# A two-layer trunk on one core: the second FFN's gate and up by seven block products

## The chip, the cores and the metric

The kernel runs on one core of a Trainium2 chip, in one launch. The metric is the device time of an execution in microseconds (us): for the kernel before, the median of three runs on the chip. In profiles PE is TensorE's matrix multiply and PEld its weight load, DVE is VectorE, ACT is ScalarE, POOL is GpSimd, and SP is SyncE, which issues the transfers (DMAs).

## The reference

A trunk of two layers on 1024 tokens with 1024 features, all in float32. Layer 0 is an S5 state-space mixer, layer 1 a dilated attention; each is followed by a SwiGLU FFN whose hidden width is 2816 (22 tiles of 128). The change touches the end of layer 1.

```python
def rmsnorm(x, g):
    xf = x.astype(jnp.float32)
    y = xf * lax.rsqrt(jnp.mean(xf * xf, axis=-1, keepdims=True) + RMS_EPS)
    return (y * g.astype(jnp.float32)).astype(x.dtype)

def swiglu(xn, w_gate_up, w_down):
    gate, up = jnp.split(xn @ w_gate_up, 2, axis=-1)
    return (jax.nn.silu(gate) * up) @ w_down

for layer in range(DEPTH):                   # 2 layers
    xn = rmsnorm(h, norm_mix[layer])
    ...                                      # y: S5 mixer, or dilated attention with x @ w_o at its end
    h = h + y.astype(h.dtype)
    h = h + swiglu(rmsnorm(h, norm_ffn[layer]), ffn_w_gate_up[layer], ffn_w_down[layer]).astype(h.dtype)
return rmsnorm(h, norm_final)
```

## The kernel before

**Number format.** Every float32 operand of a large product is split in two: a part `hi` rounded to the format fp32r, and the rest, `lo = x - hi`. ScalarE makes `hi` (a copy) and VectorE makes `lo` (a subtraction). A product is then three matmuls (`mm3`): hi·hi, hi·lo and lo·hi, from lines L244 to L246 of the profile. A matmul takes a 128x128 weight tile and a moving tile of 128x512.

**Tiling.** Activations lie feature by feature: a tile `128x1024` is one block of 128 features for all tokens, and its two halves (`hf`) are tokens 0 to 511 and 512 to 1023. Layer 1's end runs in four stages. The attention's *output projection* makes the eight feature blocks `f` of `h` (features 0 to 2 are mostly done inside the attention, whose order is planned apart); `residual` adds the old `h`, splits the sum into `HH` and `HL`, transposes it on TensorE (`ht`) and stores it by tokens in DRAM (`htok`), and collects the squares in `acc`. The *second FFN's gate and up* (`gate_up`) runs over 22 units `m`: each loads two weight tiles of 512 KB (`load_w`: transfer, GpSimd multiplies the norm's gain `g` in, ScalarE `whi`, VectorE `wlo`) and makes 2 x 2 products of 8 x 3 matmuls, 96 in all. After that VectorE multiplies by the norm factor `rb`, ScalarE takes silu, and GpSimd multiplies gate by up into `hid`, which stays on chip. In unit 0 the statistics come in: `st` sums the squares (`rstd_compact`), `rb` spreads the factor over the partitions (`rstd_bcast`). The *last down projection* (`fin`) runs over two halves of the output features and 11 chunks of two hidden tiles; `down_chunk` loads a piece of `w_down` and splits it (`dwh`, `dwl`) and the two hidden tiles (`sh`, `sl`). The *final norm* follows.

**The first FFN already works by blocks.** There `gate_up_blocks` cuts the product of a unit in 2 x 2 blocks: the weights by halves of the input features (first or second 512) and by gate or up, the activations by halves of features and of tokens. Seven block products of 4 x 3 matmuls take the place of eight: the left sides A11, A12, S1, S2, S3, A22, S4 are made for each unit by `a_blocks` (sums by GpSimd on L1037 and the lines behind it, splits by `a_split`, L1023), and the right sides B11, T1, B21, T2, T3, T4, B22 are made once, four tiles each, in the stage before (`b_first`, `b_second`, `bsplit` on L895). Of the 22 hidden tiles the first 16 are stored to DRAM and loaded again in the down projection.

**Order.** Outside the attention no order is written by hand: the program is handed to a scheduler that sets a row for each instruction on each engine, and an engine works its rows in that order. Tiles come from pools with a few buffers a tag (`whi` and `wlo` have three each), and a tile's first writer waits for the last reader of the tile that held the buffer before.

Of the kernel before, what the change touches and what calls it, by code (L numbers as in the profile page):

```python
# [18 lines left out]
NT = 8  # L19
# [151 lines left out]
def trunk(tc, a, out):  # L171
# [813 lines left out]
    def first_gu(layer):  # L985
        return [load_w(w_cols(a["ffn_w_gate_up"][layer], DFF * vg), g_ffn[layer], spare=vg == 1) for vg in range(2)]

    def gate_up(layer, acc, first=(), beside=None):
        w = a["ffn_w_gate_up"][layer]
        g = g_ffn[layer]  # L990
        first = list(first)
        hid = []
        rb = None
        for m in range(NF):
            ps = [[PB("gu") for _ in range(2)] for _ in range(2)]
            wx = []
            for vg in range(2):
                wx.append(first.pop(0) if first else load_w(w_cols(w, DFF * vg + 128 * m), g))
            st = {}
            if m == 0:  # L1000
                st = {KS: lambda: st.update(r=rstd_compact(acc, f"ffn{layer}")),
                      KR: lambda: st.update(b=rstd_bcast(st["r"], f"ffn{layer}"))}
# [10 lines left out]
            if beside and m in beside:  # L1013
                with tc.issue_after(last.ins):
                    beside[m]()
        return hid

    def a_split(name, src):
        where = ASPOT[name]
# [6 lines left out]
    ASPOT = {"A11": "whi", "S1": "wlo", "A12": "z", "S2": "z", "S3": "whi", "A22": "wlo", "S4": "z"}  # L1026

    def a_blocks(w, m):
# [9 lines left out]
        t["A11"] = a_split("A11", a11)  # L1038
        t["S1"] = a_split("S1", sf)
        G.tensor_sub(sf, sf, a11)  # L1040
        t["A12"] = a_split("A12", a12)
        t["S2"] = a_split("S2", sf)
        G.tensor_sub(a21, a11, a21)
        G.tensor_sub(a12, a12, sf)
        t["S3"] = a_split("S3", a21)
        t["A22"] = a_split("A22", a22)
        t["S4"] = a_split("S4", a12)
        return t

    def gate_up_blocks(layer, acc, beside=None):  # L1050

        w = a["ffn_w_gate_up"][layer]
# [3 lines left out]
        for m in range(NF):  # L1056
            t = a_blocks(w, m)
# [39 lines left out]
        return hid, hdram  # L1097
# [22 lines left out]
    def residual(f, ps, acc, tag, vf=(), tok=None):  # L1120
# [3 lines left out]
        for hf in range(2):  # L1124
# [8 lines left out]
            if tok is not None:  # L1133
                p = bank(tok, "ht")
# [530 lines left out]
    for m in range(NT):  # L1665
# [5 lines left out]
        for hf in range(2):  # L1671
            for k in ks_:
                o_mms(ps, w, hf, k)
# [72 lines left out]
```

## Time and profile before

| what | us |
|---|---|
| median of three runs (lowest, highest) | 2410.17 (2409.41, 2410.5) |
| the profiled execution | 2412.11 |
| its span in the trace | 2409.7 |
| the output projection, features 3 to 7 | about 1618 to 1680 |
| second FFN, gate and up: first to last matmul start | 1680.3 to 2162.5 |
| last down projection and final norm | to 2409.7 |
| first FFN, gate and up by blocks: first to last matmul start | 364.6 to 792.4 |

The profiled execution is one run of its own. All times in the rows are microseconds from the start of its span, and a row's engine is busy from its first instruction's start to its last one's end; TensorE's matmuls overlap in its pipeline, so that one shows 0.39 us while the next starts 0.23 us after it.

### The profile page before, as it was taken

Reading aid. Unit: us, or ns where it says so; the run is one execution under the profiler, and the core shown is the slowest. Engines: PE = TensorE matmul, PEld = TensorE weight load, DVE = VectorE, ACT = ScalarE, POOL = GpSimd, SP = SyncE. Lnnn points to the kernel's source line nnn. Section 1 sums busy time; section 2 is a strip of 40 time slices with the busy share of each in tenths; the row PEclk is TensorE's granted clock in tenths of the full one; section 3 lists DMA queues with packets and bytes.
Section 4 is the critical chain, followed back from the end, with each engine's and each line's share of the span. In section 5 each row is a group of like instructions: output and inputs, shape, how many; then the busy total and the mean of one; then the engine's idle time right before and its main releaser. Section 6 shows DMA issues by size and latency. Waiting matters only on the chain. (4 is left out here: it accounts for less than half of the span.)

```text
span 2409.7 us, 31977 instructions
## 1 busy us (share of the span) xinstructions
PE 2316.1 (96%) x12688; PEld 1960.4 (81%) x12688; DVE 1313.6 (55%) x2210; ACT 890.2 (37%) x1685; POOL 724.9 (30%) x581
## 2 busy tenths in 40 slices
PE   4779999999999999999999999999999999999998
PEld 3668887888888888889898989778888888888887
DVE  9994357766666435365667676656232323233434
ACT  7523334333333324255566565544111111113333
POOL 6661246666655001032112110115223222310100
PEclk9879999999999999999999999999999999999999
DMA  5213222222222521111111111324111111122112
GB/s 142 86 47 88 89 88 75 84 79 79 88 79 66 206 76 56 53 53 33 40 36 45 45 36 45 114 79 118 40 44 53 44 53 51 46 99 68 44 53 87
DMA packets 199319, 168.93 MB, mean 70 GB/s; under 512 B 18185, under 2 KB 171009, under 8 KB 199170
## 3 DMA queue, kind: packets, MB, share of 16 engines
q1 hardware_dynamic: 197154, 159.56, 20.9%
q0 software_dynamic: 2016, 7.34, 0.9%
q8 instruction: 99, 1.62, 0.3%
q14 instruction: 50, 0.41, 0.1%
HBM read 133.32 MB, written 33.55 MB: 69 GB/s over the span
## 5 line engine op out<-in xcount | busy, mean ns | idle before, releaser
L245 PE MATMUL gu<-hl,whi 128*128 128x512 f32 x704 | 274.1, 389 | 0.0
L244 PE MATMUL gu<-hh,whi 128*128 128x512 f32 x704 | 274.0, 389 | 0.0
L246 PE MATMUL gu<-hh,wlo 128*128 128x512 f32 x704 | 274.0, 389 | 0.0
L244 PE MATMUL pqk<-whi,hh 128*128 128x256 f32 x768 | 233.4, 304 | 1.2 <-ACT nat L1354 1.2
L246 PE MATMUL pqk<-whi,hl 128*128 128x256 f32 x768 | 217.4, 283 | 2.2 <-DVE hl L1132 2.2
L245 PE MATMUL pqk<-wlo,hh 128*128 128x256 f32 x768 | 217.4, 283 | 0.0
L209 ACT ACTIVATE whi<-wraw 128x1024 fp32r<-128x1024 f32 x92 | 97.1, 1059 | 312.9 <-PE gu L245 254.9
L234 POOL TENSOR_TENSOR wraw<-wraw,vec 128x1024 f32<-128x1024 f32 x46 | 88.2, 1917 | 348.0 <-DMA wraw<-in_ffn_w_gate_up_dram 197.3
L1112 DVE TENSOR_TENSOR dwl<-wraw,dwh 128x512 fp32r<-128x512 f32 x86 | 63.5, 741 | 225.5 <-ACT dwh L209 216.5
L244 PEld LDWEIGHTS pqk<-whi,hh 128*128 128x128 f32 x768 | 146.9, 191 | 18.5 <-issue 15.1
L209 ACT ACTIVATE dwh<-wraw 128x512 fp32r<-128x512 f32 x86 | 53.9, 629 | 279.4 <-PE fin L245 135.7
L244 PEld LDWEIGHTS gu<-hh,whi 128*128 128x128 f32 x704 | 132.1, 188 | 27.6
L246 PEld LDWEIGHTS gu<-hh,wlo 128*128 128x128 f32 x704 | 132.1, 188 | 27.3
L245 PEld LDWEIGHTS gu<-hl,whi 128*128 128x128 f32 x704 | 132.1, 188 | 27.3
L246 PEld LDWEIGHTS pqk<-whi,hl 128*128 128x128 f32 x768 | 146.6, 191 | 2.4 <-DVE hl L1132 2.4
L245 PEld LDWEIGHTS pqk<-wlo,hh 128*128 128x128 f32 x768 | 147.0, 191 | 0.0
L1469 DVE TENSOR_TENSOR pl<-ptp,ph 128x512 fp32r<-128x512 f32 (+1 forms) x160 | 100.2, 635 | 75.6 <-ACT ph L209 73.9
L245 PE MATMUL dn<-sl,dwh 128*128 128x512 f32 x352 | 136.6, 389 | 0.0
L244 PE MATMUL dn<-sh,dwh 128*128 128x512 f32 x352 | 135.3, 390 | 1.0 <-DVE dtmp L1126 1.0
L246 PE MATMUL dn<-sh,dwl 128*128 128x512 f32 x352 | 134.7, 389 | 0.0
L236 DVE TENSOR_TENSOR wlo<-wraw,whi 128x1024 fp32r<-128x1024 f32 x65 | 105.4, 1624 | 52.9 <-ACT whi L209 50.1
L244 PE MATMUL fin<-dwh,sh 128*128 128x512 f32 x336 | 130.7, 389 | 0.0
(1179 smaller groups left out, 5937.4 us busy)
## 6 DMA issues: line engine op xcount, KB each, us to landing
wraw<-in_ffn_w_gate_up_dram SPq DMA_DIRECT2D x88, 512.0 KB, 3.8
wraw<-in_ffn_w_down_dram SPq DMA_DIRECT2D x44, 512.0 KB, 3.3
wraw<-in_s_w_glu_dram SPq DMA_DIRECT2D x16, 512.0 KB, 4.0
hidd<-hid SPq DMA_DIRECT2D x16, 512.0 KB, 2.6
hd<-hidd SPq DMA_DIRECT2D x16, 512.0 KB, 8.1
wraw<-in_dil_w_qkv_dram SPq DMA_DIRECT2D x32, 256.0 KB, 3.3
x<-in_x_dram SPq DMA_DIRECT2D x8, 512.0 KB, 7.3
xts<-xT SPq DMA_DIRECT2D x8, 512.0 KB, 3.1
```

The source lines that it names most:

```text
L209: A.activation(o, i, AF.Copy)
L234: G.tensor_tensor(r3, r3, g.unsqueeze(2).to_broadcast([128, view[0], view[1]]), op=ALU.mult)
L236: V.tensor_sub(lo, raw, hi.bitcast(F32))
L244: T.matmul(ps, lh, rh, start=first, stop=False)
L245: T.matmul(ps, lh, rl, start=False, stop=False)
L246: T.matmul(ps, ll, rh, start=False, stop=last)
L1112: V.tensor_sub(wl, half(raw, i), wh.bitcast(F32))
L1469: V.tensor_sub(o_, i_, (t["ph"][:, :, 1] if part else t["ph"]).bitcast(F32))
```

## The change

The second FFN's gate and up go through `gate_up_blocks` as well, and `gate_up` falls away. The activations' blocks are made while the output projection runs, by the new function `residual_x` and the lines behind it. In the second layer the gain goes into the activations, the norm factor of the up half is left out in the units and multiplied in by VectorE at the end, when the down projection's result is added to `h`; 16 hidden tiles are stored and loaded again, and the down projection begins with tiles 16 to 21.

```diff
-    def first_gu(layer):
-        return [load_w(w_cols(a["ffn_w_gate_up"][layer], DFF * vg), g_ffn[layer], spare=vg == 1) for vg in range(2)]
-
-    def gate_up(layer, acc, first=(), beside=None):
-        w = a["ffn_w_gate_up"][layer]
-        g = g_ffn[layer]
-        first = list(first)
...
-        for m in range(NF):
-            ps = [[PB("gu") for _ in range(2)] for _ in range(2)]
-            wx = []
-            for vg in range(2):
...
-            unit_mms(ps, wx, HH, HL, m == 0, dict(st))
-            rb = st["b"] if m == 0 else rb
-            hd = Z4(f"hid{layer}_{m}") if m < 16 else B4(f"hid{layer}_{m}")
-            for hf in range(2):
-                s_ = T2("s_")
-                V.tensor_mul(s_, ps[hf][0], half(rb, hf))
-                last = V.tensor_mul(half(hd, hf), ps[hf][1], half(rb, hf))
-                A.activation(s_, s_, AF.Silu)
-                G.tensor_mul(half(hd, hf), half(hd, hf), s_)
-            hid.append(hd)
...
+    def a_split(name, src, layer):
+        where = ASPOT[layer][name]
         nm = uid(name)
-        t = Z4(nm, F32R) if where == "z" else whl.tile([128, 1024], F32R, tag=where, name=nm, bufs=3)
+        t = Z4(nm, F32R) if where == "z" else B4(nm, F32R) if where == "b" else whl.tile([128, 1024], F32R, tag=where, name=nm, bufs=3)
...
+    ASPOT = ({"A11": "whi", "S1": "wlo", "A12": "z", "S2": "z", "S3": "whi", "A22": "wlo", "S4": "z"},
+             {"A11": "whi", "S1": "wlo", "A12": "whi", "S2": "wlo", "S3": "whi", "A22": "wlo", "S4": "b"})
+
+    def a_blocks(layer, m):
...
+    def gate_up_blocks(layer, acc, t=None, beside=None):
...
+            t = t or a_blocks(layer, m)
...
+            V.tensor_add(half(hd, 0), do("A22", "T4"), c)
             if m == 0:
                 r = rstd_compact(acc, f"ffn{layer}")
-            V.tensor_add(half(hd, 0), do("A22", "T4"), c)
+            last = V.tensor_add(u, do("S4", "B22"), u)
             if m == 0:
                 rb = rstd_bcast(r, f"ffn{layer}")
             V.tensor_mul(s_, s_, half(rb, 0))
             A.activation(s_, s_, AF.Silu)
-            G.tensor_mul(s_, s_, half(rb, 0))
+            if layer == 0:
+                G.tensor_mul(s_, s_, half(rb, 0))
             G.tensor_mul(half(hd, 0), half(hd, 0), s_)
-            last = V.tensor_add(u, do("S4", "B22"), u)
-            G.tensor_mul(half(hd, 1), half(hd, 1), half(rb, 1))
+            if layer == 0:
+                G.tensor_mul(half(hd, 1), half(hd, 1), half(rb, 1))
             V.tensor_mul(u, u, half(rb, 1))
...
+    def residual_x(f, ps, acc, tok):
+
+        XG[f] = B4("xg")
+        for hf in range(2):
+            tmp = T2("dtmp")
+            V.tensor_add(tmp, ps[hf], half(HH[f], hf).bitcast(F32))
+            (V if f == 7 else G).tensor_add(tmp, tmp, half(HL[f], hf).bitcast(F32))
+            A.activation(half(XG[f], hf), tmp, AF.Copy, scale=g_ffn[1][:, f:f + 1])
...
-        for hf in range(2):
-            for k in ks_:
-                o_mms(ps, w, hf, k)
+        for hf, k in [(hf, k) for k in ks_ for hf in range(2)] if m == NT - 1 else [(hf, k) for hf in range(2) for k in ks_]:
+            o_mms(ps, w, hf, k)
         if m == NT - 1:
-            first = first_gu(1)
-        residual(m, ps, acc, "h2", (), obanks[m if m < OU else (OU - 1 - m) % 4][1])
+            for nm, x in (("T2", 0), ("T3", 1)):
+                for k in range(KH - 1):
+                    bsplit(nm, k, half(XG[k], x), "z")
+            first = a_blocks(1, 0)
+        residual_x(m, ps, acc, obanks[m if m < OU else (OU - 1 - m) % 4][1])
+        if m < KH:
+            bsplit("B11", m, half(XG[m], 0), "h")
+            G.tensor_sub(half(XG[m], 0), half(XG[m], 1), half(XG[m], 0))
+            bsplit("T1", m, half(XG[m], 0), "b")
+        else:
+            x, y = XG[m], XG[m - KH]
+            e = V if m == NT - 1 else G
+            bsplit("B21", m - KH, half(x, 0), "h")
+            e.tensor_sub(half(y, 0), half(x, 1), half(y, 0))
+            e.tensor_sub(half(y, 1), half(x, 1), half(y, 1))
+            G.tensor_sub(half(x, 0), half(x, 0), half(y, 0))
+    bsplit("T2", KH - 1, half(XG[KH - 1], 0), "z")
+    bsplit("T3", KH - 1, half(XG[KH - 1], 1), "z")
+    for k in range(KH):
+        bsplit("T4", k, half(XG[k + KH], 0), "z")
+    for k in range(KH):
+        bsplit("B22", k, half(XG[k + KH], 1), "z")
     at.close()
     nb["pb"] = 0
     ring = [psc, pov, pqk, ptp]
-    hid = gate_up(1, acc, first)
+    hid, hdram, rstd = gate_up_blocks(1, acc, first)
...
+    order = list(range(NS, NF, 2)) + list(range(0, NS, 2))
+    nc_ = len(order)
+    nxt = down_chunk(hid, wd, order[0], 0)
     for ch in range(2):
         ps = [PB("fin") for _ in range(8)]
         todo = []
-        for k0 in range(0, NF, 2):
-            todo += [(k0 + i, c) for i, c in enumerate(nxt)]
-            if ch == 0 or k0 < NF - 2:
-                k1 = (k0 + 2) % NF
-                nxt = down_chunk(hid, wd, k1, 512 * (ch + (k1 == 0)), ch == 1 and k1 == NF - 2)
-            if ch == 1 and k0 == NF - 4:
+        for n, k0 in enumerate(order):
+            todo += [(2 * n + i, c) for i, c in enumerate(nxt)]
+            if ch == 0 and 2 * n < NS:
+                for k in (2 * n, 2 * n + 1):
+                    hid[k] = Z4(f"hd{k}")
+                    nc.sync.dma_start(hid[k], hdram[k])
+            if ch == 0 or n < nc_ - 1:
...
-            V.tensor_add(y, ps[tt], y)
+            V.scalar_tensor_tensor(y, ps[tt], rstd[:, tt:tt + 1], y, op0=ALU.mult, op1=ALU.add)
```

**VectorE in the output projection, at the sums of feature 1.** `po` is a feature's product, `dtmp` the sum with the old `h`, `wlo` the low part of a weight tile that a transfer has just brought. Before:

```order
L236 TENSOR_TENSOR wlo_2685_15547<-wraw_2683_15545,whi_2684_15546 128x1024
L1130 TENSOR_TENSOR dtmp_2649_15307<-dtmp_2649_15307,hl_1125_6992 128x512
L1132 TENSOR_TENSOR hl_1128_7005<-dtmp_2655_15343,hh2_1094_6836 128x512 x2
L1132 TENSOR_TENSOR hl_1125_6992<-dtmp_2649_15307,hh1_1084_6768 128x512
L1126 TENSOR_TENSOR dtmp_2652_15322<-po__2592_14992,hh1_1084_6768 128x512
L236 TENSOR_TENSOR wlo_2706_15718<-wraw_2704_15716,whi_2705_15717 128x1024
```

After:

```order
L236 TENSOR_TENSOR wlo_2706_15579<-wraw_2704_15577,whi_2705_15578 128x1024
L895 TENSOR_TENSOR B11_0_2651_15301<-xg_2644_15274,B11_0_2651_15301 128x512
L1115 TENSOR_TENSOR dtmp_2655_15315<-po__2587_14971,hh1_1084_6768 128x512
L895 TENSOR_TENSOR T1_0_2652_2653_15305<-xg_2644_15274,T1_0_2652_2653_15305 128x512
L236 TENSOR_TENSOR wlo_2732_15761<-wraw_2730_15759,whi_2731_15760 128x1024
L1115 TENSOR_TENSOR dtmp_2658_15329<-po__2592_14992,hh1_1084_6768 128x512
```

The sum of feature 1's second half (from `po__2592`) stood ahead of the next `wlo`, which waits for a transfer (the last row of before); now a `wlo` is the row directly ahead of it, and the splits of the new blocks (`B11`, `T1`) stand between. The addition of `hl` into `dtmp`, done by VectorE for the first half before, has left it for GpSimd in both halves.

**VectorE behind the output projection's last product** (`dtmp` from `po__2702` or `po__2728` is the first half of feature 7). Before:

```order
L1126 TENSOR_TENSOR dtmp_2713_15784<-po__2702_15714,hh7_1225_7694 128x512
L1130 TENSOR_TENSOR dtmp_2713_15784<-dtmp_2713_15784,hl_1240_7799 128x512
L236 TENSOR_TENSOR wlo_2736_15958<-wraw_2734_15956,whi_2735_15957 128x1024
L236 TENSOR_TENSOR wlo_2739_15965<-wraw_2737_15963,whi_2738_15964 128x1024
L1132 TENSOR_TENSOR hl_1240_7799<-dtmp_2713_15784,hh7_1225_7694 128x512
L1126 TENSOR_TENSOR dtmp_2716_15799<-po__2703_15715,hh7_1225_7694 128x512
L1130 TENSOR_TENSOR dtmp_2716_15799<-dtmp_2716_15799,hl_1240_7799 128x512
L1145 TENSOR_TENSOR acc2_2643_15264<-acc2_2643_15264,dtmp_2713_15784 128x512
L1132 TENSOR_TENSOR hl_1240_7799<-dtmp_2716_15799,hh7_1225_7694 128x512
L1145 TENSOR_TENSOR acc2_2643_15264<-acc2_2643_15264,dtmp_2716_15799 128x512
```

After, the first 12 of 34 rows that end with the split of the last block, `B22_3`:

```order
L1115 TENSOR_TENSOR dtmp_2757_15862<-po__2728_15757,hh7_1225_7694 128x512
L895 TENSOR_TENSOR B21_2_2727_15751<-xg_2720_15722,B21_2_2727_15751 128x512
L1116 TENSOR_TENSOR dtmp_2757_15862<-dtmp_2757_15862,hl_1240_7799 128x512
L895 TENSOR_TENSOR T2_2_2737_2738_15819<-xg_2664_15356,T2_2_2737_2738_15819 128x512
L895 TENSOR_TENSOR T3_0_2739_2740_15822<-xg_2644_15274,T3_0_2739_2740_15822 128x512
L895 TENSOR_TENSOR T3_1_2741_2742_15825<-xg_2654_15314,T3_1_2741_2742_15825 128x512
L1115 TENSOR_TENSOR dtmp_2760_15876<-po__2729_15758,hh7_1225_7694 128x512
L895 TENSOR_TENSOR T3_2_2743_2744_15828<-xg_2664_15356,T3_2_2743_2744_15828 128x512
L1116 TENSOR_TENSOR dtmp_2760_15876<-dtmp_2760_15876,hl_1240_7799 128x512
L990 TENSOR_TENSOR S1_2749_15840<-sf_2747_15835,S1_2749_15840 128x512
L990 TENSOR_TENSOR S3_2752_15852<-wraw_2746_15833,S3_2752_15852 128x512
L990 TENSOR_TENSOR S2_2751_15847<-sf_2747_15835,S2_2751_15847 128x512
```

Before, two sums, their splits and the squares led to the FFN, whose products could begin with the features before. Now splits of blocks and of the first unit's weight blocks (`S1` to `S4`) stand between and behind the two halves of feature 7.

**ScalarE at the start of the last down projection** (`sh` is the high part of a hidden tile, `dwh` that of a weight tile). Before:

```order
L209 ACTIVATE sh_3041_18636<-hid1_2_2753_16191 128x1024
L209 ACTIVATE dwh_3043_18640<-wraw_3038_18630 128x512
L209 ACTIVATE sh_3045_18644<-hid1_3_2766_16316 128x1024
L209 ACTIVATE sh_3050_18702<-hid1_4_2779_16441 128x1024
L209 ACTIVATE dwh_3048_18698<-wraw_3047_18696 128x512
L209 ACTIVATE dwh_3052_18706<-wraw_3047_18696 128x512
L209 ACTIVATE sh_3054_18710<-hid1_5_2792_16566 128x1024
```

After:

```order
L209 ACTIVATE sh_3305_19071<-hid1_19_3206_18613 128x1024
L209 ACTIVATE sh_3312_19133<-hid1_20_3228_18752 128x1024
L209 ACTIVATE sh_3316_19141<-hid1_21_3250_18891 128x1024
L209 ACTIVATE sh_3323_19203<-hd0_3296_19053 128x1024
L209 ACTIVATE dwh_3310_19129<-wraw_3309_19127 128x512
L209 ACTIVATE dwh_3314_19137<-wraw_3309_19127 128x512
```

Before, the rows of `sh` and `dwh` alternated in the order of the tiles' use, but for one pair; now the copy of the reloaded tile `hd0` stands ahead of the weights of tiles 20 and 21.

## Rows read from the trace of the kernel before

**Rows 1.** the page's head: span, and busy time and instructions of each engine

```profile
span 2409.7 us, 31977 instructions
...
PE 2316.1 (96%) x12688; PEld 1960.4 (81%) x12688; DVE 1313.6 (55%) x2210; ACT 890.2 (37%) x1685; POOL 724.9 (30%) x581
```

**Rows 2.** busy time by stage: stretch, length, five engines (instructions), clock, DMA, GB/s

```profile
390.00:780.00 390.00, 390.00 (x1725) 323.10 (x1724) 276.49 (x343) 124.27 (x212) 239.78 (x166) 1.00 0.25 79
...
800.00:1040.00 240.00, 238.87 (x1078) 198.29 (x1076) 107.71 (x115) 85.85 (x116) 22.20 (x14) 1.00 0.23 77
...
1710.00:2160.00 450.00, 450.00 (x1987) 372.60 (x1986) 129.93 (x126) 69.07 (x86) 124.38 (x80) 1.00 0.17 49
```

**Rows 3.** tile gu: ns min/median/max, first and last start

```profile
L244 PE MATMUL gu<-hh,whi x704: 387/389/486, 1680.3 to 2162.0; 128*128 128x512 f32 x176
...
L246 PE MATMUL gu<-hh,wlo x704: 387/389/474, 1681.1 to 2162.5; 128*128 128x512 f32 x176
```

**Rows 4.** tile pB, the first FFN's products: first and last

```profile
L244 PE MATMUL pB<-B,A x176: 389/389/628, 364.6 to 781.1; 128*128 128x512 f32 x176
...
L246 PE MATMUL pB<-B,S x88: 389/389/389, 396.4 to 792.4; 128*128 128x512 f32 x88
```

**Rows 5.** TensorE in order of time, first FFN's start: start, us

```profile
377.23 1.57 PE L968 MATMUL st<-ones_c,acc 128*128 128x1 f32 x8 [2.13 <-POOL acc L962]
...
381.36 0.63 PE L245 MATMUL pT<-T,S 128*128 128x512 f32 x1
...
381.79 0.63 PE L246 MATMUL pT<-T,S 128*128 128x512 f32 x1
```

**Rows 6.** busy time around that wait; column as in Rows 2

```profile
375.00:377.20 2.20, 0.10 (x1) 0.00 (x0) 1.84 (x2) 1.88 (x4) 2.20 (x3) 1.00 0.00 0
...
379.00:381.00 2.00, 2.00 (x10) 1.96 (x10) 1.03 (x3) 0.00 (x0) 1.47 (x1) 0.50 0.00 0
...
383.00:385.00 2.00, 2.00 (x7) 1.56 (x6) 0.11 (x1) 0.00 (x0) 0.00 (x0) 0.65 0.57 167
```

**Rows 7.** VectorE in order of time, first FFN's start

```profile
368.16 0.69 DVE L1023 TENSOR_TENSOR S<-sf,S 128x512 fp32r<-128x512 f32 x1
...
368.77 0.68 DVE L1023 TENSOR_TENSOR A<-wraw,A 128x512 fp32r<-128x512 f32 x1
...
395.64 1.78 DVE L1023 TENSOR_TENSOR S<-wraw,S 128x512 fp32r<-128x512 f32 x1
```

**Rows 8.** the chain that ended last, stretch 1600:1720: start, us

```profile
1625.98 4.11 DMA wraw<-in_dil_w_o_dram
...
1640.12 0.44 PE ht L1136 x4
...
1695.02 1.68 PE st L968 x16
...
1703.21 0.87 PE rb L981 x8
```

**Rows 9.** ScalarE, GpSimd and TensorE in order of time, output projection

```profile
1630.17 1.06 ACT L209 ACTIVATE whi<-wraw 128x1024 fp32r<-128x1024 f32 x1 [2.94 <-DMA wraw<-in_dil_w_o_dram]
...
1629.14 1.29 POOL L1130 TENSOR_TENSOR dtmp<-dtmp,hl 128x512 f32<-128x512 f32 x1 [5.46 <-DVE dtmp L1126]
...
1617.98 0.39 PE L244 MATMUL po__2660_15372<-oh,whi 128*128 128x512 f32 x1
...
1632.80 0.50 PE L244 MATMUL po__2681_15543<-oh,whi 128*128 128x512 f32 x1 [0.51 <-ACT ht L209]
```

**Rows 10.** ScalarE in order of time, start of the first down projection

```profile
819.80 0.63 ACT L209 ACTIVATE dwh<-wraw 128x512 fp32r<-128x512 f32 x1 [3.86 <-PE dn L245]
...
820.34 1.04 ACT L209 ACTIVATE sh<-hd 128x1024 fp32r<-128x1024 f32 x1
```

**Rows 11.** tile hd: issues of the reloads and their landing

```profile
L1158 SPq DMA_DIRECT2D hd<-hidd x16: 319/320/432, 773.8 to 799.9; - x16
...
DMA to landing us min/median/max: 3.3/8.1/11.2
```

More of the change, by code (lines that the diff above doesn't have):

```diff
@@ L1024, in a_split @@
         return t
-    ASPOT = {"A11": "whi", "S1": "wlo", "A12": "z", "S2": "z", "S3": "whi", "A22": "wlo", "S4": "z"}
-    def a_blocks(w, m):
+    ASPOT = ({"A11": "whi", "S1": "wlo", "A12": "z", "S2": "z", "S3": "whi", "A22": "wlo", "S4": "z"},
+             {"A11": "whi", "S1": "wlo", "A12": "whi", "S2": "wlo", "S3": "whi", "A22": "wlo", "S4": "b"})
+    def a_blocks(layer, m):
+        w = a["ffn_w_gate_up"][layer]
         raw = []
@@ L1096, in gate_up_blocks @@
                     beside[m]()
-        return hid, hdram
+            t = None
+        return hid, hdram, r
     def down_chunk(src, w, k0, c0, spare=False):
@@ L1118, in down_chunk, with residual @@
         return r
-    def residual(f, ps, acc, tag, vf=(), tok=None):
+    def residual(f, ps, acc, tag, vf=()):
         wide = B4("dtmp") if f % 2 == 0 else None
@@ L1132, in residual @@
             V.tensor_sub(half(HL[f], hf), tmp, half(HH[f], hf).bitcast(F32))
-            if tok is not None:
-                p = bank(tok, "ht")
-                for b in range(4):
-                    T.transpose(p[:, 128 * b:128 * b + 128], tmp[:, 128 * b:128 * b + 128], ident)
-                tt_ = T2("ht")
-                copy(tt_, p)
-                nc.sync.dma_start(htok[4 * hf:4 * hf + 4, :, 128 * f:128 * f + 128].rearrange("b t c -> t b c"),
-                                  tt_.rearrange("t (b c) -> t b c", b=4))
             if f == 0:
@@ L1145, in residual @@
                 (V if f == 7 or f in vf else G).tensor_add(half(acc, hf), half(acc, hf), tmp)
+    def residual_x(f, ps, acc, tok):
[5 more added lines that the diff above has]
+            A.activation(half(XG[f], hf), tmp, AF.Copy, scale=g_ffn[1][:, f:f + 1])
+            p = bank(tok, "ht")
+            for b in range(4):
+                T.transpose(p[:, 128 * b:128 * b + 128], tmp[:, 128 * b:128 * b + 128], ident)
+            tt_ = T2("ht")
+            copy(tt_, p)
+            nc.sync.dma_start(htok[4 * hf:4 * hf + 4, :, 128 * f:128 * f + 128].rearrange("b t c -> t b c"),
+                              tt_.rearrange("t (b c) -> t b c", b=4))
+            if f == 0:
+                A.activation(half(acc, hf), tmp, AF.Square)
+            else:
+                A.activation(tmp, tmp, AF.Square)
+                (V if f == 7 else G).tensor_add(half(acc, hf), half(acc, hf), tmp)
     def down_feature(src, hdram, w, acc, tag, pre=lambda: None):
@@ L1693, in trunk @@
         todo = []
-        for k0 in range(0, NF, 2):
-            todo += [(k0 + i, c) for i, c in enumerate(nxt)]
-            if ch == 0 or k0 < NF - 2:
-                k1 = (k0 + 2) % NF
-                nxt = down_chunk(hid, wd, k1, 512 * (ch + (k1 == 0)), ch == 1 and k1 == NF - 2)
-            if ch == 1 and k0 == NF - 4:
+        for n, k0 in enumerate(order):
[5 more added lines that the diff above has]
+            if ch == 0 or n < nc_ - 1:
+                n1 = (n + 1) % nc_
+                nxt = down_chunk(hid, wd, order[n1], 512 * (ch + (n1 == 0)), ch == 1 and n1 == nc_ - 1)
+            if ch == 1 and n == nc_ - 2:
                 continue
-            edge = k0 == 0 or k0 == NF - 2
+            edge = n == 0 or n == nc_ - 1
             for tt, (k, c) in [(tt, kc) for tt in range(8) for kc in todo] if edge else [(tt, kc) for kc in todo for tt in range(8)]:
```

34 lines of the change are left out of this document (9 added, 25 removed).

## The prediction

> **What bounds the kernel now.** I read the page's head first: TensorE is busy for 2316.1 of the span's 2409.7 us and no other engine for much more than half of it [rows 1]. An average says little of one stage, so the busy times of the stages come next [rows 2]. In the second FFN's gate and up, from 1710 to 2160, TensorE is busy for all of 450.00 us, VectorE for 129.93 and GpSimd for 124.38, at the full clock level (1.00 granted, 2.4 GHz). The first FFN's same stage, which already works by blocks, shows 390.00 of 390.00 us for TensorE, and its VectorE (276.49) and GpSimd (239.78) are far from full. So both forms of this stage are bounded by the number of matmuls, as long as what feeds them comes in time. The edges of the stage are what has to be looked at by hand.
>
> **Products left out.** The tile view gives the products' first and last start, 1680.3 and 2162.5 us: 482.2 us for 22 units of 96 matmuls, 2112 in all [rows 3]. The statistics stand among them: `st` takes 1.68 and `rb` 0.87 us in the chain of waits [rows 8]. That leaves 479.65 / 2112 = 0.2271 us a matmul. By blocks a unit has 84, so 264 fall away: **−60.0 us**. A second way to the number is the first FFN: its 1848 products run from 364.6 to 792.4, 427.8 us [rows 4], and 482.2 − 427.8 = 54.4 us. The two differ by 5.6 us, which the first FFN lost at its start: it waited 2.13 us for GpSimd before `st` [rows 5], and afterwards the granted clock was 0.50 and then 0.65 [rows 6], with matmuls 0.43 us apart [rows 5]. I take −60.0 and put the start's losses into terms of their own.
>
> **The units between.** The order puts the splits of unit m+1's weight blocks among unit m's rows on VectorE, 16 rows a unit as in the first FFN, and GpSimd has two multiplications a unit fewer. The first FFN's 390 full microseconds are the cover; I charge nothing. The new part is that the blocks of all units take turns in three `whi` and three `wlo` buffers; if that makes units wait, the price is a rival below.
>
> **Output projection, feature 1.** VectorE's row for the sum of feature 1's second half now stands behind a `wlo`, and the addition of `hl` behind it is GpSimd's. In the trace, that weight's transfer was issued at 1625.98 and took 4.11 us [rows 8], so `whi` ran at 1630.17 for 1.06 [rows 9]. Then come `wlo` (twice the elements of a split of 0.61, [rows 7]: 1.2), the sum (0.6) and GpSimd's addition (1.29, [rows 9]): 1631.3 + 1.2 + 0.6 + 1.3 = 1634.4. TensorE reaches the transposes of that sum after 48 matmuls of feature 3, which began at 1617.98 [rows 9]: 10.9 us and, by 0.44 each, three groups of transposes [rows 8] make 1630.2 and 1630.6 with a fourth. Behind the transposes on TensorE stand all products of the next feature, so it waits 3.8 us. Before, it waited 0.51 us at that place [rows 9], which falls away: **+3.3**, between 0 (the transfer starts earlier since its buffer does) and 5 (GpSimd is late by its own next row).
>
> **Behind the output projection.** Take the end of its last product as zero. From the sum of feature 7 to `B22_3` VectorE has 34 rows, and the FFN's first unit can't end before the last of them. In the first FFN's start, splits that run alone follow each other 0.61 us apart (368.16, 368.77), and one that runs beside GpSimd took 1.78 in place of 0.68 [rows 7]. Thirty-three rows at 0.61 and a small one of 128x8 (0.2 at most) are 20.3 us. GpSimd has some 14 instructions in that stretch (differences of blocks, the sums for the next units' weight blocks, products of the first unit), and if each of them delays one VectorE row by 1.78 − 0.68 = 1.1, 15.4 come on top: 35.7 us. TensorE has there 98 matmuls of units 0 and 1 that the order puts ahead of `B22_3`'s, 22.3 us, five groups of transposes, 2.2, `st`, 1.7, and half of `rb`, 0.4: 26.6 us. The difference is **+9.1**. It is bounded by 0 (no delay: 20.3 is less than 26.6) and by 25 (all rows but four at 1.7, 52 us). I take the middle since half of VectorE's rows have a GpSimd instruction beside them. The old start, two sums and two splits, waited for nothing that the chain shows but `st` and `rb` [rows 8], so nothing is given back.
> The Trainium skill ("SBUF — State Buffer", section "Who interferes with whom") has a VectorE instruction with two SBUF inputs and a GpSimd instruction that reads SBUF exclude each other for their whole length. Rows 7 agree (0.68 alone, 1.78 beside GpSimd). Without that rule the sum of this paragraph would be 0 and the time near 2359; by it, 2368.
>
> **The clock.** The wait of 2.13 us before the first FFN's `st` left a granted clock of 0.50 (the level of 1.2 GHz) and 0.65 (partly that) in the stretches after it [rows 5, 6]. From 379 to 385 that is about 0.5, 0.5 and 0.35 of 2 us each that were lost, 2.7. VectorE's waits come in pieces here, with matmuls between; I charge one such loss, **+3**, between 0 and 8.
>
> **Last down projection.** The weights `dwh` of tiles 20 and 21, the third chunk, stand on ScalarE behind the copy of the reloaded `hd0`. That copy needs a `sh` buffer that the products of tile 19 must free first; when they have, the copy takes 1.04 and a `dwh` 0.63 [rows 10], then VectorE's `dwl` about as long as a split that runs alone (0.61). That makes 2.3 in which TensorE has only the end of tile 19's products: **+2**, between 0 and 4. The reloads are hidden: in the first FFN's end the same 16 were issued from 773.8 to 799.9 and landed in 3.3 to 11.2 us [rows 11], and the stage behind is busy for 238.87 of 240.00 us [rows 2]. The multiplication by the norm factor at the end goes into the addition that VectorE does anyway, one instruction for one; nothing is charged.
>
> **Sum.** The profiled execution took 2412.1 us, 2.4 more than its span. 2412.1 − 60.0 + 3.3 + 9.1 + 3 + 2 = 2369.5. The median of the runs is 1.9 below that execution: **2367.6**, said as 2368.
>
> **Rivals.**
> *Starts as cheaply as the first FFN's.* The whole difference is then the one measured between the sister stages, 54.4, and with the down projection's 2 the time is 2410.2 − 52.4 = 2358. For it: that start too makes blocks late on VectorE. Against it: there the blocks of its features were spread over the stage before, and here 34 rows are left for the time after the last product.
> *The clock stays at its lower level through the starved stretch.* Matmuls come 0.43 apart [rows 5] at that level: 98 × 0.43 + 4.3 = 46.4 us of TensorE's work in place of 26.6. It, not VectorE's 35.7, then ends the stretch: 19.8 in place of 9.1 + 3, or 2375. For it: one wait of 2.13 was followed by a fall to 0.50 [rows 5, 6]. Against it: there the clock was back at 1.00 by 390 [rows 2].
> The Trainium skill ("TensorE: Matmul & The Clock Gate", section "HAM oscillation — how this bites in real kernels") describes waits for data that come again and again, each with its own fall of the clock; this is the rival that it favours, and the trace of before shows one such fall only.
> *Units wait for buffers.* With three and three buffers a unit's first blocks can't be made until the last unit's are read; 0.5 to 1 us in each of 21 units makes 2378 to 2389.
> *Slower than before.* If the blocks of a unit can be made only after the unit before has ended, each unit waits for a GpSimd sum (1.3, as in [rows 9]), a copy (0.63, [rows 10]) and a split (0.68 to 1.78, [rows 7]), about 3.3 us: 21 × 3.3 = 69 and 2368 + 69 = 2437. It decides from 42.6 / 21 = 2.0 us a unit on. Against it: in the first FFN four of the seven blocks go through the same buffers and TensorE never waits [rows 2].
> *No change.* The products left out would have to be hidden behind something else; with TensorE at 450 of 450 us nothing is there to hide them.
>
> **Chances.** The forecast 0.61, the cheap start 0.13, the slow clock 0.15, waits for buffers 0.05, slower 0.04, no change 0.02. The forecast's own range is 2359 to 2378: the feature 1 term at 0 and the start at 3, or the start at 19. With the cheap start and the slow clock around it the range is 2356 to 2383. Two runs of this kernel that differ by 0.2% (4.8 us) are told apart, not less. Faster by more than that: 0.61 + 0.13 + 0.15 + 0.05 = 0.94; within it 0.02; slower 0.04.
>
> **What would show it.** Right: products of the second FFN over some 420 + 14 us from first to last; between the last product of `po` and unit 1 TensorE waits, and mostly for VectorE's splits (`B21_3`, `T2_3`, `T4`, `B22`) and for the transposes of feature 7; the transposes of feature 1 wait about 4 us behind a `wlo`; a wait of some 2 us at the third chunk of `fin`; units of 84 × 0.2271 = 19.1 us each with no wait. Wrong: GpSimd's instructions delay fewer VectorE rows than 14, so that the start costs nothing; or units longer than 19.1 us, with `whi` or `wlo` waiting for TensorE; or a granted clock below 1.00 in the middle of the stage.

## The result and the profile after

| | before | after |
|---|---|---|
| median of four runs each, us | 2409.79 | 2366.84 (2366.45 to 2372.97) |
| span of the profiled execution, us | 2409.7 | 2365.2 |
| ratio to before, 95% interval | | 0.983 (0.9812 to 0.9848) |

The change saves 43.0 us where 42.6 were forecast, and the median lies 1.2 us below the prediction's 2368. Runs of one kernel scatter by 2 to 11 us (e3 and e8 below), more than the 4.8 us that the prediction took as told apart, so below a few us I read the profiled executions, stretch by stretch.

The head of the page after, against [rows 1]:

```profile
span 2365.2 us, 32123 instructions
PE 2259.1 (96%) x12424; PEld 1910.8 (81%) x12424; DVE 1471.7 (62%) x2437; ACT 964.1 (41%) x1845; POOL 796.1 (34%) x646
```

TensorE's share is as before; it has 57 us less to do. Where the time went is read from the tile views (median duration, first and last start). `pB` now covers both FFNs, so its first start is the first FFN's and its last the second's:

```profile
L244 PE MATMUL pB<-B,A x352: 389/389/792, 364.9 to 2105.3; 128*128 128x512 f32 x176
L246 PE MATMUL pB<-B,S x176: 389/389/395, 384.8 to 2116.6; 128*128 128x512 f32 x176
...
L244 PE MATMUL dn<-sh,dwh x352: 389/389/500, 787.9 to 1027.9; 128*128 128x512 f32 x176
...
L244 PE MATMUL fin<-dwh,sh x336: 389/389/500, 2116.8 to 2355.9; 128*128 128x512 f32 x168
```

(The first and second line come from one tile, the third and fourth from one each.) `dn` is the first down projection. Three stretches follow from the starts. The first FFN's products, 364.9 to the first `dn` at 787.9, take 423.0 us; before they took 427.8 and a matmul's pitch, 428.0 [rows 4]. That is 5.0 us which the prediction didn't have. From the first `dn` to the first `fin` it is 787.9 to 2116.8, 1328.9 us; before, from 792.6 to the last product of `gu` at 2162.5 and a pitch, 1370.1 [rows 3, 4]. That is −41.2 where the prediction had −60.0 + 3.3 + 9.1 + 3 = −44.6. From the first `fin` to the last matmul it is 1.7 us more than before. All of it: −5.0 − 41.2 + 1.7 and 0.3 either way at the ends of these stretches make the span's −44.5 us.

The middle stretch begins with layer 1's attention, for which the prediction had no term. The change's own part begins with the first product of the output projection's feature 3, before at 1617.98 [rows 9], after here:

```profile
1611.24 0.39 PE L244 MATMUL po__2674_15392<-oh,whi 128*128 128x512 f32 x1
```

From there to the first `fin` it is 505.6 us; before, to the same point at 2162.7, 544.7. That is −39.1 against the forecast −44.6, and the other −2.1 lie ahead of it, in the attention.

TensorE's waits from 1600 to 1760 after (what waits, for whom: us in total, times, longest):

```profile
PE ht L1120 <- POOL dtmp L1116: 7.8, 3, 4.2
PE ht L1120 <- DVE dtmp L1116: 4.3, 2, 3.8
PE pT L244 <- ACT S L209: 1.2, 1, 1.2
PE pB L245 <- DVE B L895: 0.9, 1, 0.9
PE pB L244 <- ACT B L209: 0.2, 1, 0.2
```

The transposes `ht` wait for sums (at feature 1, and behind the projection at features 6 and 7), and some products for splits. No product of `B22` waits. In order of time (start, us, engine, instruction, in brackets the idle time ahead of it and its releaser):

```profile
1627.90 1.11 PE L1120 MATMUL ht<-cst,dtmp 128*128 128x128 f32 x4 [4.21 <-POOL dtmp L1116]
...
1685.59 1.11 PE L1120 MATMUL ht<-cst,dtmp 128*128 128x128 f32 x4 [3.01 <-POOL dtmp L1116]
...
1697.68 1.09 PE L1120 MATMUL ht<-cst,dtmp 128*128 128x128 f32 x4 [3.85 <-DVE dtmp L1116]
```

The first is the wait at feature 1, 4.21 us. All others lie between 1681 and 1698, soon after the last product of the output projection (it starts at 1676.4 and the next matmul at 1676.6), and sum to 10.2 us. Busy times of these stretches (columns as in [rows 2]):

```profile
1628.00:1632.00 4.00, 4.00 (x15) 3.35 (x16) 0.72 (x2) 2.86 (x6) 3.08 (x3) 0.67 0.53 160
1684.00:1688.00 4.00, 1.91 (x5) 1.00 (x5) 1.08 (x1) 2.29 (x4) 4.00 (x5) 0.66 0.21 66
1688.00:1692.00 4.00, 2.34 (x6) 1.22 (x6) 4.00 (x4) 2.86 (x6) 4.00 (x3) 0.50 0.22 66
1692.00:1696.00 4.00, 1.22 (x2) 0.50 (x2) 4.00 (x4) 0.56 (x2) 4.00 (x3) 0.50 0.21 66
1696.00:1700.00 4.00, 2.32 (x8) 2.06 (x9) 2.13 (x3) 1.15 (x3) 2.09 (x3) 0.50 0.00 0
1700.00:1704.00 4.00, 4.00 (x15) 3.15 (x14) 3.46 (x6) 4.00 (x8) 0.85 (x1) 0.71 0.25 76
1740.00:2100.00 360.00, 360.00 (x1590) 298.20 (x1589) 251.40 (x306) 113.19 (x190) 161.64 (x114) 1.00 0.26 78
```

The clock column is at 0.50 (1.2 GHz) or partly so in two places: behind the wait at feature 1, and from the wait of 3.01 us on until after 1700, through the third long wait. Busy time times what is missing to 1.00 gives what that cost: 0.6 + 1.2 + 0.6 + 1.2 + 1.2 behind the output projection and 1.3 behind feature 1, 6.1 us. The last row is the middle of the stage: full, at 1.00.

What VectorE did there, and GpSimd:

```profile
1683.13 0.69 DVE L1115 TENSOR_TENSOR dtmp<-po__2728_15757,hh 128x512 f32<-128x512 f32 x1 [1.80 <-POOL acc L1129]
1686.91 1.63 DVE L895 TENSOR_TENSOR B<-xg,B 128x512 fp32r<-128x512 f32 x1 [3.10 <-ACT B L209]
1688.47 1.76 DVE L1116 TENSOR_TENSOR dtmp<-dtmp,hl 128x512 f32<-128x512 f32 x1
1690.16 5.10 DVE L895 TENSOR_TENSOR T<-xg,T 128x512 fp32r<-128x512 f32 x3
...
1713.47 2.48 DVE L895 TENSOR_TENSOR B<-xg,B 128x512 fp32r<-128x512 f32 x4
```

```profile
1684.29 1.25 POOL L1116 TENSOR_TENSOR dtmp<-dtmp,hl 128x512 f32<-128x512 f32 x1
...
1689.65 1.72 POOL L1006 TENSOR_TENSOR sf<-wraw 128x512 f32<-128x512 f32 x1
1691.32 1.71 POOL L1129 TENSOR_TENSOR acc<-acc,dtmp 128x512 f32<-128x512 f32 x1
```

First VectorE waits for GpSimd, which is busy without a gap (in the second row by way of ScalarE); from 1687 to 1696 both have work, and each instruction takes about 1.7 us in place of 0.61 (VectorE's pitch alone) or 1.25 (GpSimd's time alone). The last row of VectorE is the four splits of `B22`, done at 1715.9, 39.3 us after the projection's end (1676.6).

### The profile page after: what moved, and what is told of

Its sections match the earlier page's. It is cut to its first block, busy times and chain, and to the rows that moved or that the text cites. A ratio compares the mean times of both kernels' runs of the same rounds, so it can differ in the third digit from the quotient of the medians.

```text
span 2365.2 us, 32123 instructions
## 1 busy us (share of the span) xinstructions
PE 2259.1 (96%) x12424; PEld 1910.8 (81%) x12424; DVE 1471.7 (62%) x2437; ACT 964.1 (41%) x1845; POOL 796.1 (34%) x646
## 5 line engine op out<-in xcount | busy, mean ns | idle before, releaser
L244 PE MATMUL pT<-T,S 128*128 128x512 f32 x528 | 206.6, 392 | 1.2 <-ACT S L209 1.2
L246 PE MATMUL pT<-T,S 128*128 128x512 f32 x528 | 206.2, 391 | 0.9 <-DVE S L990 0.9
L245 PE MATMUL pT<-T,S 128*128 128x512 f32 x528 | 206.4, 391 | 0.0
L990 DVE TENSOR_TENSOR A<-wraw,A 128x512 fp32r<-128x512 f32 x132 | 138.7, 1063 | 75.0 <-ACT A L209 74.4
L245 PE MATMUL pB<-B,A 128*128 128x512 f32 x352 | 137.4, 390 | 0.9 <-DVE B L895 0.9
L244 PE MATMUL pB<-B,A 128*128 128x512 f32 x352 | 137.6, 391 | 0.2 <-ACT B L209 0.2
L246 PE MATMUL pB<-B,A 128*128 128x512 f32 x352 | 137.2, 390 | 0.0
L245 PE MATMUL fin<-dwl,sh 128*128 128x512 f32 x336 | 130.7, 389 | 0.0
L246 PE MATMUL fin<-dwh,sl 128*128 128x512 f32 x336 | 129.6, 389 | 0.0
```

The source lines that it names most:

```text
L244: T.matmul(ps, lh, rh, start=first, stop=False)
L245: T.matmul(ps, lh, rl, start=False, stop=False)
L246: T.matmul(ps, ll, rh, start=False, stop=last)
```

## Experiments

Each edit is one to the changed kernel unless it says otherwise. "Waits" are TensorE's; a stretch "`dn` to `fin`" is the one of 1328.9 us above. Each is read from one profiled execution, and it scatters: e7, whose edit stands behind this stretch, shows 1329.7. So differences of about 1 us (e2, e6) are not told apart.

**e1: the first FFN in the old order** (the sum over `T4` in the first layer stands behind `rstd_compact` again, too). The 5.0 us there were not in the prediction.

```diff
-            last = V.tensor_add(u, do("S4", "B22"), u)
+            if layer:
+                last = V.tensor_add(u, do("S4", "B22"), u)
             if m == 0:
                 rb = rstd_bcast(r, f"ffn{layer}")
...
             G.tensor_mul(half(hd, 0), half(hd, 0), s_)
+            if layer == 0:
+                last = V.tensor_add(u, do("S4", "B22"), u)
```

> The changed kernel with the first FFN's units written in the old order again (the product of S4 and B22 behind the norm factor); nothing else differs in what is computed. The changed kernel's trace ends its first FFN's products 4.7 us earlier than before, without a wait ahead of the statistics and without the fall of the clock there; this was not in the prediction. Theory one, the new order did it: the wait of about 2 us for GpSimd and the fall to 0.50 come back, first matmul of the first down projection near 792.6, time near 2371.5. Theory two, it is chance which of VectorE and GpSimd gets in first there, and the order has no part in it: the wait may or may not be in the trace, and the median stays within 1 us of 2366.8 over several runs or scatters by 3 to 5.

Median 2371.35 us (2366.09 to 2374.57), span 2367.6. The first FFN's products take 427.0 us. GpSimd after (first fence) and in e1 (second):

```profile
369.21 2.28 POOL L1009 TENSOR_TENSOR sf<-sf,wraw 128x512 f32<-128x512 f32 x1 [9.67 <-DVE S L990]
```

```profile
367.85 6.48 POOL L1009 TENSOR_TENSOR sf<-sf,wraw 128x512 f32<-128x512 f32 x1 [9.70 <-DVE S L990]
374.29 3.46 POOL L962 TENSOR_TENSOR acc<-acc,hn 128x512 f32<-128x512 f32 x2
```

In e1 one GpSimd sum took 6.48 us while VectorE had a run of two-input instructions, so that the squares behind it came late, and `st` waited 2.1 us again, as before ([rows 5], 2.13). Theory one is borne out in this profile, but see e8 and e11.

**e2: the low part of the first token half added by VectorE**, as before the change.

```diff
-            (V if f == 7 else G).tensor_add(tmp, tmp, half(HL[f], hf).bitcast(F32))
+            (V if f == 7 or hf == 0 else G).tensor_add(tmp, tmp, half(HL[f], hf).bitcast(F32))
```

> The changed kernel with the addition of the low part for the first token half given back to VectorE in features 0 to 6, as it was before (7 instructions leave GpSimd). The prediction's theory, VectorE's 34 rows and their delays set the end of the start: a row more for VectorE in that stretch costs 0.6 to 1.8 us, the wait for the transposes of feature 1 falls by 1.3, sum 2366 to 2368. Rival from the changed kernel's trace, GpSimd's queue is what is late (it is busy without a gap from 1676 to 1696, and the transposes wait 7.8 us for its additions): the wait at feature 1 falls from 4.2 to 2 or 3, those at features 5 and 6 from 3.6 to 1 or 2, with less time at the lower clock level, sum 2361 to 2364.

Median 2366.37 us, span 2364.1; `dn` to `fin` 1.0 us less. The wait at feature 1 stayed (3.8), those of the transposes at features 6 and 7 fell from 7.9 to 5.2, and a new one of 2.8 us stood at `pT`, for VectorE's split of `S`. The rival's size was wrong: one addition a feature less on GpSimd moves TensorE's wait along. The median is what the prediction's theory expected, but the wait at feature 1 fell by 0.4 and not by 1.3.

**e3: no splits of T4 and B22**. Products take other tiles in their place, so the output is another one.

```diff
-        bsplit("T4", k, half(XG[k + KH], 0), "z")
+        spots["T4", k] = spots["T1", k]
...
-        bsplit("B22", k, half(XG[k + KH], 1), "z")
+        spots["B22", k] = spots["B21", k]
```

> The changed kernel without the splits of T4 and B22: the products take T1's and B21's tiles in their place, so the output is another one; 8 rows each of VectorE and ScalarE are left out behind the output projection, the matmuls are as many. The prediction's theory, the last split B22_3 sets when the first unit can end: 8 rows of 0.61 to 1.7 us are 4.9 to 13 us, and the whole excess of 9.1 is about covered: 2357 to 2362. Rival, the waits lie at the start of the stretch (transposes of features 5 to 7, first products) and nothing waits for T4 and B22: within 1.5 us of the changed kernel, 2365.3 to 2368.3.

Median 2365.49 us, span 2363.3. The tile views' first starts:

```profile
L244 PE MATMUL dn<-sh,dwh x352: 387/389/496, 787.4 to 1027.5; 128*128 128x512 f32 x176
...
L244 PE MATMUL fin<-dwh,sh x336: 389/389/389, 2116.7 to 2354.0; 128*128 128x512 f32 x168
```

`dn` to `fin` is 1329.3 us: eight rows less on VectorE and on ScalarE there are worth nothing. (The down projection is 1.7 us shorter, since its wait went with another order of rows, as in e7.) The prediction's theory of the start falls.

**e4: the norm factor in the units again.**

```diff
-            if layer == 0:
-                G.tensor_mul(s_, s_, half(rb, 0))
+            G.tensor_mul(s_, s_, half(rb, 0))
...
-            V.scalar_tensor_tensor(y, ps[tt], rstd[:, tt:tt + 1], y, op0=ALU.mult, op1=ALU.add)
+            V.tensor_add(y, ps[tt], y)
```

> The changed kernel with the norm factor of the up half multiplied in within the units again, by two GpSimd instructions a unit (44 in all), and a plain addition at the end. The prediction charged nothing for this part either way, since the first FFN's stage is full with those instructions in it: 2365.8 to 2367.8, units of 19.1 us without a wait. Rival, GpSimd is late at the edges and these instructions come on top there: 2 to 5 us slower, 2369 to 2372, with a wait in unit 0 or 1.

Median 2367.58 us, span 2365.3. The middle of the stage, GpSimd 219.13 us in place of 161.64, is as full as ever:

```profile
1740.00:2100.00 360.00, 360.00 (x1590) 298.16 (x1589) 237.73 (x307) 114.61 (x192) 219.13 (x154) 1.00 0.25 78
```

This part of the change gives and costs nothing.

**e5: GpSimd's work of features 5 to 7 on VectorE.**

```diff
-            (V if f == 7 else G).tensor_add(tmp, tmp, half(HL[f], hf).bitcast(F32))
+            (V if f >= 5 else G).tensor_add(tmp, tmp, half(HL[f], hf).bitcast(F32))
...
-            e = V if m == NT - 1 else G
+            e = V if m >= 5 else G
...
-            G.tensor_sub(half(x, 0), half(x, 0), half(y, 0))
+            e.tensor_sub(half(x, 0), half(x, 0), half(y, 0))
```

(and the squares' addition alike)

> The changed kernel with GpSimd's work of features 5 to 7 in the output projection (additions of the low part and of the squares, three differences of blocks a feature) on VectorE, where feature 7 had most of it already: 15 instructions change engine, nothing else. The prediction's theory, VectorE's rows set the end of the start: 15 more rows of 0.61 are up to 9 us more, less some delays by GpSimd, 2368 to 2376. Rival from the changed kernel's trace and the run before: VectorE's two-input instructions and GpSimd's take turns there (1.7 us each while both have work), so that the stretch is as long as the sum of both, and an instruction that costs 0.61 on VectorE in place of 1.27 on GpSimd shortens it: 15 x 0.66 = 10 us less work, of 10 us of waits 4 to 8 fall away, with one or two us of the lower clock: 2358 to 2363.

Median 2363.68 us (2361.47 to 2365.11), span 2363.3; `dn` to `fin` 2.6 us less. The median lies 0.7 above the rival's range and below the theory's. VectorE, with 15 rows more, is not later: where GpSimd is idle its rows follow each other 0.60 apart. The waits behind the projection are 7.3 us in place of 10.2, the largest part for ScalarE's copies of `S`:

```profile
PE pT L244 <- ACT S L209: 2.9, 3, 1.7
PE pT L244 <- ACT T L209: 2.0, 2, 1.5
```

One of the few sums that GpSimd kept is why:

```profile
1690.61 4.66 POOL L1009 TENSOR_TENSOR sf<-sf,wraw 128x512 f32<-128x512 f32 x1 [4.84 <-DVE S L990]
```

**e6: feature 7's weight behind feature 1's sum on VectorE.** `behind` is the sum of feature 1's second half, for feature 7's weight alone.

```diff
-        V.tensor_sub(lo, raw, hi.bitcast(F32))
+        with tc.issue_after(behind.ins):
+            V.tensor_sub(lo, raw, hi.bitcast(F32))
```

> The changed kernel with VectorE's row for the low part of feature 7's weight tile held behind the sum of feature 1's second half; nothing else. If that row is what makes the transposes of feature 1 wait (4.2 us in the changed kernel, and 1.3 us in which the clock is back at its lower level after it), the wait falls to 1 or less and the time to 2361 to 2364. Rival, the transposes are late because GpSimd now adds the low part in both halves, one behind the other (1.3 us each) and behind the squares: the wait falls by 1.5 at most, 2365 to 2367.

Median 2365.64 us, span 2363.8; the wait at feature 1 is 3.1 us in place of 4.2, `dn` to `fin` 0.8 less. The time is the rival's, but the cause is not GpSimd. VectorE (first) and ScalarE (second) there:

```profile
1622.32 0.69 DVE L899 TENSOR_TENSOR T<-xg,T 128x512 fp32r<-128x512 f32 x1 [3.75 <-ACT T L209]
1622.92 0.68 DVE L1121 TENSOR_TENSOR dtmp<-po__2592_14992,hh 128x512 f32<-128x512 f32 x1
```

```profile
1620.70 1.06 ACT L209 ACTIVATE whi<-wraw 128x1024 fp32r<-128x1024 f32 x1 [3.53 <-DMA wraw<-in_dil_w_o_dram]
1621.67 0.61 ACT L209 ACTIVATE T<-xg 128x512 fp32r<-128x512 f32 x1
```

ScalarE waits for the transfer with `whi`, the copy of `T1` stands behind it, and VectorE's split of `T1` stands ahead of the sum. So the `wlo` made 1.1 of the 4.2 us, and the transfer holds the sum up by this second way too.

**e7: the reloaded tiles' copies behind the weights of tiles 20 and 21.** For the first reloaded pair alone; `wcopy` holds ScalarE's copies `dwh`.

```diff
-            copy(sh, src[k0 + i])
+            with tc.issue_after(wcopy[-i - 2].ins):
+                copy(sh, src[k0 + i])
```

> The changed kernel with ScalarE's copy of the first two reloaded tiles in the last down projection held behind the weights of the chunk before (tiles 20 and 21); nothing else. The prediction's theory: the wait of 1.4 us at the third chunk goes, first to last matmul of the down projection 239.2 in place of 240.9, time 2365. Rival, the copy is then late itself, since it stands behind a row that waits for a transfer: a wait of the same length one chunk later, 2366.8.

Median 2365.11 us, span 2364.0. The wait of 1.4 us is gone, and the down projection takes 239.1 us in place of 240.9, as long as before the change.

**e8: e5, e6 and e7 together.**

> The three edits above together: GpSimd's work of features 5 to 7 on VectorE, the weight behind the sum, the copy of the reloaded tiles behind the weights. If each takes away a wait of its own, their gains add up: 4 to 8, 3 to 5 and 1.5, sum 2353 to 2359. If TensorE only waits for the same chain of VectorE and GpSimd at another place, the first two give no more than the better of them: 2360 to 2363.

Median 2360.69 us (2357.38 to 2368.49), span 2359.6; `dn` to `fin` 1321.2 us, 7.7 less than after, and the down projection 1.7 less. The median is in the range of the second expectation, but the first FFN, which the edits don't touch, took 426.9 us, 3.9 more than after: its GpSimd sum shows 6.48 us here too, and `st` waited.

```profile
368.43 6.48 POOL L1013 TENSOR_TENSOR sf<-sf,wraw 128x512 f32<-128x512 f32 x1 [9.70 <-DVE S L994]
```

So the new order doesn't keep that from happening.

**e9: feature 7's weight behind feature 1 on both engines.** As e6, and `behind[0]` is ScalarE's scaled sum of feature 1:

```diff
-        copy(hi, raw)
+        with tc.issue_after(behind[0].ins):
+            copy(hi, raw)
```

> The changed kernel with both rows of feature 7's weight tile held back: ScalarE's copy behind its row for the scaled sum of feature 1, VectorE's low part behind that sum. In the run with VectorE's row alone held back the wait at feature 1's transposes fell only from 4.2 to 3.1: VectorE still waited 3.75 us for ScalarE's copy of T1, which stood behind ScalarE's copy of that weight, which waited 3.4 us for the transfer. If the transfer reaches TensorE over ScalarE's queue, the wait now goes to 0 to 1 us with the 1.3 us of lower clock, span 2360 to 2362. Rival, GpSimd's row of two additions and a difference is late by itself: a wait of 2 to 3 us stays, span 2363.

Median 2363.15 us, span 2362.4; `dn` to `fin` 3.1 us less. Waits from 1600 to 1640:

```profile
PE ht L1128 <- ACT ht L209: 0.8, 1, 0.8
PE ht L1128 <- POOL dtmp L1124: 0.4, 1, 0.4
```

The 4.2 us are gone but for 1.2, most of it for the bank that the last transposes left. With e6 this shows that most of the wait came over ScalarE's queue.

**e10: as e5, and the four sums of unit 0's weight blocks on VectorE.**

```diff
+        e = V if layer and not m else G
-        G.tensor_add(sf, a21, a22)
+        e.tensor_add(sf, a21, a22)
```

(and the three differences behind it alike)

> The kernel of e5 with the four sums of unit 0's weight blocks on VectorE as well, so that GpSimd has next to nothing from feature 5's end to unit 1. In e5 one of these sums took 4.66 us on GpSimd while VectorE had a run of rows, and TensorE then waited 2.9 us for the copies of S. Theory, the two engines hold each other up: those waits fall by 2 to 4 us, span 2359 to 2361. Rival, VectorE is now what is late, with four more rows: span 2363 to 2366.

Median 2361.55 us, span 2359.3; `dn` to `fin` 1322.8 us, 6.1 less than after and 3.5 less than e5. VectorE's rows stay 0.60 apart, 19 more than after, two of them here:

```profile
1693.32 0.69 DVE L1010 TENSOR_TENSOR sf<-sf,wraw 128x512 f32<-128x512 f32 x1
1693.92 0.69 DVE L1117 TENSOR_TENSOR dtmp<-dtmp,hl 128x512 f32<-128x512 f32 x1
...
1707.72 1.90 DVE L895 TENSOR_TENSOR B<-xg,B 128x512 fp32r<-128x512 f32 x3
```

The last split of `B22` is done 32.9 us after the projection's end (1676.7), in place of 39.3, and TensorE's waits behind the projection are 5.0 us in place of 10.2. By the prediction's own prices that was to be expected too: 19 rows more are at most 19 × 0.61 = 11.6 us, and up to 15.4 of delays go. So e10 shows that GpSimd's part costs time, and only e3 tells which rows TensorE waits for.

**e11: as e1, with the last squares ahead of the first FFN on VectorE.**

```diff
-                G.tensor_add(half(acc, hf), half(acc, hf), half(hn, hf))
+                (V if m == NT - 1 else G).tensor_add(half(acc, hf), half(acc, hf), half(hn, hf))
```

> The kernel of e1 (the first FFN's units in the old order) with the additions of the last feature's squares ahead of the first FFN on VectorE in place of GpSimd. In e1 and in the kernel before TensorE waited 2.1 us there for GpSimd, which was held up by VectorE (a sum of 1.3 us took 6.5), and one kernel in the new order showed the same. If that wait is what the first FFN's start lost, its products take about 423 us in the old order too, span 2363 to 2365. Rival, the old order itself is slower: 427 us as in e1, span 2367 to 2369.

Median 2367.12 us, span 2364.6. The first FFN's products take 424.0 us in the old order, 3.0 less than in e1, with no wait of `st`. The wait for GpSimd's squares was most of what that start lost. The sum that took 6.48 us in e1 took still longer here, and TensorE waited 1.3 us for ScalarE's copy of its result, about what the 424.0 are above the changed kernel's 423.0:

```profile
368.04 9.48 POOL L1009 TENSOR_TENSOR sf<-sf,wraw 128x512 f32<-128x512 f32 x1 [9.72 <-DVE S L990]
```

**e12: all mends** (e7, e9, e10 and e11's line on the squares, in the new order).

> All mends together on the changed kernel: the work of features 5 to 7 and the sums of unit 0 on VectorE, feature 7's weight behind feature 1 on both engines, the reloaded tiles' copies behind the weights, the last squares ahead of the first FFN on VectorE. If each wait goes for itself: 3 to 6 at the start of the second FFN, 4 to 5 at feature 1, 1.7 in the down projection and the scatter of the first FFN's start, median 2352 to 2357. If the first two only move TensorE's wait along: 2358 to 2361.

Median 2353.53 us, ratio to before 0.9779 (0.9756 to 0.9802), span 2352.1: the best version. `dn` to `fin` is 1318.7 us, 10.2 less than after (e9's 3.1 and e10's 6.1 are 9.2 of it), and the down projection 1.7 less. Of the waits, 1.1 us are left at feature 1 and 5.5 behind the projection:

```profile
PE pB L250 <- ACT B L209: 2.4, 2, 1.4
PE pT L250 <- ACT S L209: 2.4, 2, 1.3
PE ht L1135 <- ACT ht L209: 0.7, 1, 0.7
```

They are for ScalarE's copies now. The median is in the range of the expectation that each wait goes for itself.

## Why the prediction came out right, and where it did not

**Products, −60.0: right.** Unit after unit is 84 matmuls in 19.04 us (from 1790.42 to 1809.46 by the first product of `B22`, below), and TensorE is full from 1740 to 2100. The rivals on buffers and on lost prefetch are out, and so is any worth of the two multiplications left out (e4).

```profile
1790.42 0.39 PE L244 MATMUL pB<-B,S 128*128 128x512 f32 x1
...
1809.46 0.39 PE L244 MATMUL pB<-B,S 128*128 128x512 f32 x1
```

**Feature 1, +3.3: right in size, its chain half right.** Measured 4.21 less the 0.51 of before, 3.7. The chain ran over a weight's transfer, but mainly by ScalarE's `whi` and the copy of `T1` behind it, which I hadn't looked at (e6, e9).

**Behind the projection, +9.1: measured 10.2, by another mechanism.** The step that failed is the one that let VectorE's last split set the time ("the FFN's first unit can't end before the last of them"). No product waited for that last split, and without it and seven others nothing changes (e3). VectorE needed 39.3 us in place of 35.7, but not as a backlog of 34 rows: it stood idle for GpSimd first, and of the delayed rows there are some eight, not 14. What TensorE waited for is at the start of the stretch, where few products are ready: the sums of features 6 and 7, which come through GpSimd and VectorE in turns, for 7.9 of the 10.2 us. Of the waits that the prediction named as signs, those for feature 7's transposes came (4.3 us), those for `B21_3`, `T2_3`, `T4` and `B22` did not. Taking GpSimd out gives 6.1 us with 19 rows more on VectorE (e10). How much of that is the end of taking turns, and how much that an instruction alone costs 0.61 on VectorE against 1.25 on GpSimd, no run here separates.

**The clock, +3: under-sized.** 6.1 us, since the waits came in two places and the second in pieces over 17 us. The rival in which the clock stays low was near in that, but TensorE's products still didn't bound the stretch: it idled for 10.2 us of it. The Trainium skill ("TensorE: Matmul & The Clock Gate", section "HAM oscillation — how this bites in real kernels") describes waits for data that come again and again, each with a fall of the clock behind it. The trace agrees in part: there is a fall behind the wait of 4.21 us (0.67) and one behind that of 3.01 (0.66, then 0.50), but the third wait, 3.85, lies inside the second fall. The prediction's remark that the trace of before shows one such fall only was a misreading: in its attention, too, TensorE waits for 8.1 of 100 us and the clock is below 1.00:

```profile
1500.00:1600.00 100.00, 91.93 (x622) 75.30 (x621) 62.10 (x168) 53.86 (x120) 12.79 (x26) 0.93 0.32 104
```

**Last down projection, +2: right.** 1.44 us of wait, 1.7 in length, and e7 shows the row that made it:

```profile
2140.19 2.11 PE L244 MATMUL fin<-dwh,sh 128*128 128x512 f32 x8 [1.44 <-ACT dwh L209]
```

**Not foreseen, −5.0: the first FFN.** I read the diff's new order there and charged nothing. In the profile of before, the wait of 2.13 us and the low clock behind it [rows 5, 6] were in plain sight as something that another order could lift. How much of the 5.0 belongs to the order stays open: both profiles in the old order with GpSimd's squares (before, e1) show the wait, and of ten in the new order one does (e8).

**The sum: luck in part.** In the change's own stretch, feature 3 to `fin`, the sum was 5.5 us too good (−44.6 against −39.1); 0.4, 1.1 and 3.1 of that are the three terms above, and 0.9 is unexplained. The attention was 2.1 us shorter than before, with no term for it and no run that tells why, and the first FFN 5.0. That these nearly cancel is luck.

## What to carry to other kernels

Count matmuls for the middle of a stage, and read its edges by who is queued behind whom, on every engine of the chain: a transfer that one row waits for reaches all rows behind it, on ScalarE as on VectorE. Where VectorE and GpSimd both have two-input work on a path that TensorE waits for, try giving it to VectorE alone: here it was 0.6 us an instruction (e10), against 1.7 on each while they took turns. And when a sum comes out right, check its terms by stretches all the same.

## What the hardware showed

A run of VectorE's two-input instructions can keep GpSimd out: a GpSimd sum that takes 1.25 us alone took 6.48 beside such a run (e1, e8, and before the change), 9.48 in e11 and 4.66 in e5. It need not: from 1687 to 1696 after the change both had runs, took turns, and each instruction took 1.7. Which of the two happens differs between executions of the same rows: the changed kernel and e8 have the same rows on every engine up to the output projection, the sum started 0.76 and 0.79 us behind VectorE's first split of `S`, and it took 2.28 in one and 6.48 in the other, with the first FFN 3.9 us longer. What decides it no run here shows.
